# Split projections: a block's products with the high weights first, those with the low weights last

## The chip, the cores and the metric

One core of a Trainium2 chip runs the whole program. The metric is the device time of one execution in microseconds. Before the change it is 2193.56 us, the median of three runs (2186.81 to 2194.06).

## The reference

Two transformer-like blocks run one after the other on 256 rows of 1024 features, in 32-bit floats. The first block normalises its input and multiplies it with one wide matrix `w_in`; the parts feed an attention of eight heads, a gated delta rule of eight heads (short convolutions, and a triangular inverse in each chunk) and gates. Output projections, a gated feed-forward network of width 2816 and a small side embedding follow. The second block has two layers with 256 rows of context beside the 256 rows of input. Its first layer projects to a state-space scan and to a convolution of 31 taps (value times the sigmoid of a gate, then the taps per channel); its second layer is a gated linear recurrence in both directions. After each comes a mixture of 16 experts with a router. A normalisation ends it.

What matters here is the common core of all of these, a projection of rows x with weights W:

```python
y = x @ W      # x: 256 or 512 rows, K = 256 to 2816; W: K x N, all 32-bit floats
```

## The kernel before

**The split.** TensorE multiplies fp32r operands. To keep more digits, both operands of a projection are split into a high part (the value rounded to fp32r) and a low part (the value less its high part), and three of the four products are summed in one PSUM tile: high x by high W, low x by high W, high x by low W. `mm3` (L294 to L299) issues the three for one K tile of 128, one behind the other.

**Loading.** `load_split` (L262) fetches weights by one DMA of 512 KB on SP's queue into a tile `raw` (128 x 1024), copies it to `wh` on ScalarE (L271), and subtracts `wh` from it into `wl` (L276), on VectorE for two of three tiles and on GpSimd for the third. `wh` and `wl` have three buffers each, `raw` six. Such a tile holds four K tiles of two column blocks for the first kind of projection below (K = 1024), two K tiles of 512 columns for the second, so a group of work takes two or more of them.

**Two kinds of projection.** `proj_fm_steps` (L301) makes features by rows: 128 columns of W are the stationary operand and the rows x (T = 256 or 512) the moving one. It takes two blocks of 128 columns at a time when K is 1024: both halves of the weights are loaded, block 0 runs its eight K tiles of three products (24), block 1 its 24, then a consumer evicts each block. With T = 256 both blocks share a PSUM tile, with T = 512 each has its own. In all it makes 46 such pairs at T = 256: 20 in the first block's `w_in`, 22 in the feed-forward network and 4 in the last layer. `proj_tm_steps` (L327) makes rows by features: 128 rows of x are stationary and 512 columns of W move; for each K tile the loop goes over two or four row tiles, each with a PSUM tile of its own. It issues 608 triples of products in the program. The experts' own products run elsewhere (L2008 on), and the thin projections call `mm3` directly.

**Steps as filler.** Both are generators that yield after each `mm3`. Most callers run them through at once. Three draw steps in between other work. In the first block the triangular inverse runs in 6 levels by 4 groups (L663): four small matmuls, `fill()` (three steps of waiting projections), a ScalarE copy of their result, four matmuls on it, `fill()`, a predicated copy on VectorE, four transposes, `fill()`, another copy; the last level has no transposes, so there are 68 fills. In the state-space scan each of 16 chunk steps draws four steps of the z projection (L1297). In the second layer's output projection, normalisation pieces are put in between the steps (L1388).

**The order of the work.** The text gives each engine's instructions a priority, and the framework lays each engine's order out beforehand, by that priority and by the times at which it expects operands. So an instruction from further down stands ahead where an earlier one was expected late. On the chip each engine then runs its list strictly in that order. Writes to the same PSUM tile keep the order of the text. Convolution taps of the state-space layer are queued and placed a few at a time directly behind named instructions (`tick`, L972): 5 behind each subtraction on VectorE, 8 behind each eviction of a value block (L1101).

Of the kernel before, what the change touches and what calls it, by code (L numbers as in the profile page):

```python
# [18 lines left out]
P = 128  # L19
# [124 lines left out]
class Net:  # L144
# [149 lines left out]
    def mm3(self, out, lh, ll, rh, rl, start, stop):  # L294
# [3 lines left out]
        mm(out, lh, rl, start=False, stop=False)  # L298
        return mm(out, ll, rh, start=False, stop=stop)  # L299

    def proj_fm_steps(self, W, c0, nblk, x, T, consumer, tag="mm", bufs=3):  # L301


        K = W.shape[0] // P
        nb = 16 // K
        Wv = W.rearrange("(k p) n -> p k n", p=P)
        for b0 in range(0, nblk, nb):
            n = min(nb, nblk - b0)
            w = self.load_split(Wv[:, :, c0 + b0 * P:c0 + (b0 + n) * P], K, n * P)
            per = 512 // T  # L310
            ps = [self.psum(tag, bufs) for _ in range(-(-n // per))]
            for b in range(n):
                o = (b % per) * T
                s = slice(b * P, (b + 1) * P)
                for k in range(K):
                    wh, wl = w(k)
                    xh, xl = x(k)
                    yield self.mm3(ps[b // per][:, o:o + T], wh[:, s], wl[:, s], xh, xl, k == 0, k == K - 1)
            for b in range(n):
                o = (b % per) * T  # L320
                consumer(b0 + b, ps[b // per][:, o:o + T])
# [9 lines left out]
    def proj_tm_steps(self, W, c0, ncol, x, tiles, consumer, tag="mm", bufs=3, last=None, after=None):  # L331


        K = W.shape[0] // P
        Wv = W.rearrange("(k p) n -> p k n", p=P)
        for n0 in range(0, ncol, 512):
            ps = {t: self.psum(tag if i < 3 else "mx", bufs) for i, t in enumerate(tiles)}
            ws = {}
            end = last is not None and n0 + 512 >= ncol
            cut = K - LAST_K if end else K  # L340

            def products(k, t):
                if k not in ws:
                    kn = min(4, K - k)
                    w = self.load_split(Wv[:, k:k + kn, c0 + n0:c0 + n0 + 512], kn, 512)
                    ws.update({k + i: w(i) for i in range(kn)})
                ts = slice(t * P, (t + 1) * P)
                xh, xl = x(k)
                return self.mm3(ps[t], xh[:, ts], xl[:, ts], *ws[k], k == 0, k == K - 1)
            for k in range(cut):  # L350
                for t in tiles:
                    yield products(k, t)
            for group in last if end else (tiles,):
                for k in range(cut, K):
                    for t in group:
                        yield products(k, t)
                for t in group:
                    consumer(t, n0, ps[t])
                if after:
                    after(n0 // 512, group)  # L360
# [2182 lines left out]
```

## Time and profile before

| | |
|---|---|
| median of three runs | 2193.56 us |
| profiled execution | 2195.8 us, span 2194.0 us |
| mean granted TensorE clock | 0.959 |
| TensorE busy | 2011.8 us, 92% |
| VectorE busy | 1101.2 us, 50% |
| ScalarE busy | 870.1 us, 40% |
| GpSimd busy | 668.5 us, 30% |

The busy time of TensorE (PE) counts modelled ends of pipelined products: one with 512 columns stands as 0.39 us in a row, while the next starts 0.23 us later. So the distance between starts tells how fast products run, and the idle time in brackets tells how long the engine stood still and for what. PEld is the loading of the stationary operand, which runs beside the products. In an operand's name `uh`, `fh`, `ev0h` are high parts of x and `ul`, `fl`, `ev0l` low ones; L297 is high by high. In proj_fm L298 is low x by high W; in proj_tm the stationary operand comes first in `mm3`, so there L298 carries the low weights and L299 the low x.

### The profile page before, as it was taken

The numbers are of one execution on the slowest core, as the hardware profiler recorded it, in microseconds if no ns is written. First come the engines' busy times: TensorE is split into PE (matmuls) and PEld (weight loads), VectorE is DVE, ScalarE is ACT, GpSimd is POOL, SyncE is SP. The second block draws the span as 40 slices with busy tenths as digits, with TensorE's granted clock in tenths as the row PEclk, the third lists the DMA queues.
The fourth block names the chain that finished last, engine by engine and source line by source line (L and its number), as shares of the span: only waits on it lengthen the run. The fifth ranks groups of instructions, "written<-read, shape, count | busy, mean of one in ns | idle before, by whom it ended". The sixth has DMA issues, their size and how long they took to land. (4 is left out here: it accounts for less than half of the span.)

```text
span 2194.0 us, 29919 instructions
## 1 busy us (share of the span) xinstructions
PE 2011.8 (92%) x11360; PEld 1449.9 (66%) x11360; DVE 1101.2 (50%) x1980; ACT 870.1 (40%) x1407; POOL 668.5 (30%) x527
## 2 busy tenths in 40 slices
PE   7999999989999878999989799998899999799996
PEld 6799877779976655677768636663487666644342
DVE  6655453554435774796466523331625565633322
ACT  5554355453334443565554123230335555311111
POOL 1413322224432275525655322221312223201110
PEclk9999999999999989999999799999999999899998
DMA  7534556667675024231124699998645234989993
GB/s 227 157 107 138 152 165 198 216 194 230 222 238 168 20 74 111 78 106 49 41 96 137 230 354 347 372 362 325 226 137 180 88 105 154 325 301 395 395 343 135
DMA packets 282845, 433.13 MB, mean 197 GB/s; under 512 B 33722, under 2 KB 159290, under 8 KB 282432
## 3 DMA queue, kind: packets, MB, share of 16 engines
q1 hardware_dynamic: 261696, 407.17, 55.3%
q10 hardware_dynamic: 16528, 10.12, 1.7%
q0 software_dynamic: 4464, 13.79, 1.7%
q8 instruction: 94, 1.54, 0.3%
q14 instruction: 63, 0.52, 0.1%
HBM read 420.17 MB, written 9.54 MB: 196 GB/s over the span
## 5 line engine op out<-in xcount | busy, mean ns | idle before, releaser
L271 ACT ACTIVATE wh<-raw 128x1024 fp32r<-128x1024 f32 x288 | 303.4, 1057 | 390.3 <-PE mm L298 146.1
L276 POOL TENSOR_TENSOR wl<-raw,wh 128x1024 fp32r<-128x1024 f32 x92 | 223.2, 2426 | 623.9 <-ACT wh L271 573.8
L276 DVE TENSOR_TENSOR wl<-raw,wh 128x1024 fp32r<-128x1024 f32 x196 | 257.5, 1316 | 298.1 <-ACT wh L271 295.1
L2017 PE MATMUL mm<-we,xs 128*64 128x512 f32 x832 | 197.4, 618 | 12.0 <-DVEq L2178 9.4
L2017 PEld LDWEIGHTS mm<-we,xs 128*64 128x64 f32 x832 | 62.2, 142 | 136.1 <-issue 119.0
L2033 DVE TENSOR_TENSOR hh<-mm,hh 128x512 f32<-128x512 f32 x19 | 13.1, 692 | 210.9 <-PE mm L2017 148.5
L1144 DVE SCALAR_TENSOR_TENSOR cf<-us,cols,cf 128x200 f32<-128x200 f32 (+14 forms) x180 | 106.9, 659 | 0.1
L1132 POOL TENSOR_TENSOR cf<-cf,cfp 128x241 f32<-128x241 f32 (+14 forms) x120 | 93.2, 812 | 35.6 <-ACT cfp L1130 35.6
L2032 ACT ACTIVATE hh<-mm 128x512 f32<-128x512 f32 x22 | 13.1, 598 | 223.5 <-PE mm L2017 161.3
L297 PE MATMUL mm<-fh,wh 128*128 128x256 f32 x352 | 100.9, 287 | 0.0
L299 PE MATMUL mm<-fh,wl 128*128 128x256 f32 x352 | 99.9, 284 | 0.9 <-POOL wl L276 0.9
L298 PE MATMUL mm<-fl,wh 128*128 128x256 f32 x352 | 99.5, 283 | 0.0
L297 PE MATMUL mm<-uh,wh 128*128 128x256 f32 x320 | 97.0, 303 | 0.0
L299 PE MATMUL mm<-uh,wl 128*128 128x256 f32 x320 | 92.4, 289 | 1.8 <-DVE wl L276 1.5
L298 PE MATMUL mm<-ul,wh 128*128 128x256 f32 x320 | 91.9, 287 | 0.0
L2003 POOL TENSOR_TENSOR h<-h,yz 128x512 f32<-128x512 f32 x16 | 24.8, 1555 | 219.6 <-DVE yz L2002 219.4
L916 PE MATMUL mx<-mraw,cs 128*32 128x256 f32 x768 | 72.7, 399 | 7.4 <-DMA mraw<-in_mod_w 7.4
L299 PE MATMUL mm<-ev0h,wl 128*128 128x512 f32 x160 | 65.1, 408 | 14.0 <-DVE wl L276 13.9
L297 PEld LDWEIGHTS mm<-fh,wh 128*128 128x128 f32 x352 | 67.4, 191 | 5.4 <-issue 5.4
L297 PE MATMUL mm<-ev0h,wh 128*128 128x512 f32 x160 | 66.0, 414 | 5.3 <-DVE c L1183 4.3
L299 PEld LDWEIGHTS mm<-fh,wl 128*128 128x128 f32 x352 | 67.4, 192 | 1.6 <-POOL wl L276 1.4
L298 PEld LDWEIGHTS mm<-fl,wh 128*128 128x128 f32 x352 | 67.5, 192 | 0.0
(968 smaller groups left out, 5236.8 us busy)
## 6 DMA issues: line engine op xcount, KB each, us to landing
mraw<-in_mod_w SPq DMA_DIRECT2D x96, 512.0 KB
we<-in_moe_w_gate SPq DMA_DIRECT2D x37, 1024.0 KB
raw<-in_w_in SPq DMA_DIRECT2D x72, 512.0 KB
we<-in_moe_w_down SPq DMA_DIRECT2D x35, 1024.0 KB
we<-in_moe_w_up SPq DMA_DIRECT2D x32, 1024.0 KB
we<-in_moe_w_up SPq DMA_DIRECT2D x52, 512.0 KB
we<-in_moe_w_down SPq DMA_DIRECT2D x46, 512.0 KB
we<-in_moe_w_gate SPq DMA_DIRECT2D x42, 512.0 KB
```

The lines of the kernel that those rows point to most:

```text
L271: ins = nc.scalar.activation(hi, raw, AF.Copy)
L276: ins = eng.tensor_tensor(lo, raw, hi.bitcast(F32), ALU.subtract)
L297: mm(out, lh, rh, start=start, stop=False)
L298: mm(out, lh, rl, start=False, stop=False)
L299: return mm(out, ll, rh, start=False, stop=stop)
L916: nc.tensor.matmul(ps[32 * g:32 * g + 32, d:d + 256], self.cs[:, k, :], w[:, g, :], start=(k == 0), stop=(k == 7))
L1132: nc.gpsimd.tensor_tensor(a, a, s, ALU.add)
L1144: yield lambda a=a, s=s, j=j: nc.vector.scalar_tensor_tensor(a, s, w(j), a, op0=ALU.mult, op1=ALU.add)
L2003: (nc.gpsimd if d else nc.vector).tensor_tensor(x[:, t, ds], x[:, t, ds], z, ALU.add)
L2017: nc.tensor.matmul(out[r], x[0][:, k, r], w, start=start, stop=stop)
L2032: nc.scalar.activation(hh, pg[2 * i], AF.Silu)
L2033: nc.vector.tensor_tensor(hh, pg[2 * i + 1], hh, ALU.mult)
```

## The change

In proj_fm a block now runs all K tiles with the high weights first (high x and low x, through the new helper `mm3_high`), and then all K tiles with the low weights. It yields after each pair but the last, and once after the low products, so as often as before: seven steps of two products and one of ten. In proj_tm the same is done inside one K tile, over the row tiles: two products with the high weights for each row tile, then one with the low weights for each. The number of steps stays. Weights are loaded and consumers called at the same places of the text.

```diff
+    def mm3_high(self, out, lh, rh, rl, start):
+        self.nc.tensor.matmul(out, lh, rh, start=start, stop=False)
+        return self.nc.tensor.matmul(out, lh, rl, start=False, stop=False)
...
+                out = ps[b // per][:, o:o + T]
                 for k in range(K):
-                    wh, wl = w(k)
-                    xh, xl = x(k)
-                    yield self.mm3(ps[b // per][:, o:o + T], wh[:, s], wl[:, s], xh, xl, k == 0, k == K - 1)
+                    ins = self.mm3_high(out, w(k)[0][:, s], *x(k), k == 0)
+                    if k < K - 1:
+                        yield ins
+                for k in range(K):
+                    ins = self.nc.tensor.matmul(out, w(k)[1][:, s], x(k)[0], start=False, stop=(k == K - 1))
+                yield ins
...
-            def products(k, t):
+            def products(k, group):
                 if k not in ws:
...
-                ts = slice(t * P, (t + 1) * P)
-                xh, xl = x(k)
-                return self.mm3(ps[t], xh[:, ts], xl[:, ts], *ws[k], k == 0, k == K - 1)
+                mm = self.nc.tensor.matmul
+                wh, wl = ws[k]
+                xh, xl = [[v[:, t * P:(t + 1) * P] for t in group] for v in x(k)]
+                for i, t in enumerate(group):
+                    mm(ps[t], xh[i], wh, start=(k == 0), stop=False)
+                    ins = mm(ps[t], xl[i], wh, start=False, stop=False)
+                    if i < len(group) - 1:
+                        yield ins
+                for i, t in enumerate(group):
+                    ins = mm(ps[t], xh[i], wl, start=False, stop=(k == K - 1))
+                yield ins
             for k in range(cut):
-                for t in tiles:
-                    yield products(k, t)
+                yield from products(k, tiles)
             for group in last if end else (tiles,):
                 for k in range(cut, K):
-                    for t in group:
-                        yield products(k, t)
+                    yield from products(k, group)
```

## Rows read from the trace of the kernel before

**Rows 1.** Page part 1: engine, busy us (share of the span), instructions.
```profile
PE 2011.8 (92%) x11360; PEld 1449.9 (66%) x11360; DVE 1101.2 (50%) x1980; ACT 870.1 (40%) x1407; POOL 668.5 (30%) x527
```

**Rows 2.** Timeline in the inversion, all engines: start, us, line, out<-in, [idle before].
```profile
149.98 0.37 PE L297 MATMUL mm<-uh,wh 128*128 128x256 f32 x1
...
150.26 0.60 ACT L673 ACTIVATE U<-g 128x512 f32<-128x512 f32 x1 [0.37 <-PE g L670]
...
151.89 0.36 PE L297 MATMUL mm<-uh,wh 128*128 128x256 f32 x1
...
152.17 0.75 DVE L678 COPY_PREDICATED V<-k_first,g 128x512 f32<-128x512 uint8 x1 [1.14 <-PE g L676]
...
152.33 0.28 PE L297 MATMUL mm<-uh,wh 128*128 128x256 f32 x1
...
152.45 0.28 PE L298 MATMUL mm<-ul,wh 128*128 128x256 f32 x1
...
153.04 0.60 PE L682 MATMUL tr<-k_main,V 128*128 128x128 f32 x4
```

**Rows 3.** Timeline of PE around its longest wait for a low part.
```profile
788.04 0.39 PE L297 MATMUL mm<-ev0h,wh 128*128 128x512 f32 x1
788.26 0.39 PE L298 MATMUL mm<-ev0l,wh 128*128 128x512 f32 x1
802.58 0.80 PE L299 MATMUL mm<-ev0h,wl 128*128 128x512 f32 x1 [13.92 <-DVE wl L276]
...
813.57 0.39 PE L298 MATMUL mm<-ev1l,wh 128*128 128x512 f32 x1
813.80 0.39 PE L299 MATMUL mm<-ev1h,wl 128*128 128x512 f32 x1
```

**Rows 4.** Line 276: what its engines waited for, then who waited for it.
```profile
  ACT wh L271: 868.8, 174
...
  PE mm L299: 2.1, 1
...
  PE mm L299: 18.9, 7
```

**Rows 5.** Waits of PE: line, waited for, us in total, times, longest.
```profile
PE mm L299 <- DVE wl L276: 15.4, 2, 13.9
...
PE tr L1243 <- POOL xw L1241: 5.8, 6, 2.4
...
PE mm L299 <- POOL wl L276: 3.5, 5, 1.5
```

**Rows 6.** Line 299: weight loads, ns min/median/max.
```profile
L299 PEld LDWEIGHTS mm<-wh,ul x128: 187/188/330, 228.5 to 372.4; 128*128 128x128 f32 x128
```

**Rows 7.** Timeline of DVE in the same stretch.
```profile
792.09 0.68 DVE L1101 TENSOR_TENSOR us<-mm,cfg 128x512 f32<-128x512 f32 x1
792.69 8.21 DVE L1144 SCALAR_TENSOR_TENSOR cf<-us,cols,cf 128x248 f32<-128x248 f32 x8
800.82 1.71 DVE L276 TENSOR_TENSOR wl<-raw,wh 128x1024 fp32r<-128x1024 f32 x1
...
805.05 1.21 DVE L276 TENSOR_TENSOR wl<-raw,wh 128x1024 fp32r<-128x1024 f32 x1
```

**Rows 8.** Timeline of ACT in the same stretch.
```profile
791.85 1.06 ACT L271 ACTIVATE wh<-raw 128x1024 fp32r<-128x1024 f32 x1 [4.78 <-DMA raw<-in_ab_w_in]
```

**Rows 9.** Stretch behind the wait: busy us by engine, PEclk, DMA share, GB/s.
```profile
802.50:814.00 11.50, 11.42 (x44) 9.37 (x45) 7.26 (x14) 3.32 (x5) 2.14 (x3) 0.87 0.45 137
```

**Rows 10.** Groups by line in 470 to 690 us: busy, mean ns, idle before.
```profile
L271 ACT ACTIVATE wh<-raw 128x1024 fp32r<-128x1024 f32 x68 | 71.9, 1059 | 120.8 <-PE mm L298 64.4 <-PE mm L299 38.9 <-issue 12.7
...
L276 POOL TENSOR_TENSOR wl<-raw,wh 128x1024 fp32r<-128x1024 f32 x22 | 52.7, 2398 | 107.6 <-ACT wh L271 107.6
```

**Rows 11.** Groups by line in 117 to 235 us, PE.
```profile
L676 PE MATMUL g<-V,U 128*128 128x128 f32 x168 | 22.4, 276 | 0.0
...
L682 PE MATMUL tr<-k_main,V 128*128 128x128 f32 x76 | 11.7, 277 | 0.1
```

## The prediction, made before the result was known

> **What bounds the kernel now.** I read the page's busy times first, then the waits of TensorE over the whole span, then the line of the subtraction that makes the low weights, then the timeline at its longest wait. The reader is to see this. TensorE is busy 92% of the span, and has as many weight loads as products [rows 1], so the time is first of all a count of products. Products of the split projections are issued 0.12 us apart at 256 columns (152.33 to 152.45 us, [rows 2]) and 0.23 us apart at 512 (813.57 to 813.80, [rows 3]), whichever of the three operand pairs they carry. What the change can touch beside the count is time in which TensorE stands still for a low part: 18.9 us in 7 waits, as seen from the subtraction's line [rows 4], and 13.9 us of that is one wait [rows 5]. Everything else that TensorE waits for is named by other lines.
>
> **The change part by part.** Times are summed on the profiled execution, 2195.8 us (span 2194.0 and 1.8 around it); the median of the three timed runs is 2193.56, 2.2 below, and I subtract that at the end.
>
> (a) Count. No product, subtraction, copy, DMA or eviction is added or removed. A block of eight K tiles still has 24 products. At equal spacing that is 0 us.
>
> Here a rule of the Trainium skill speaks against the change. In proj_tm the stationary operand is the row slice of x: before, the high slice served two products in a row; after, the other slice comes between. The row to look at is 11360 loads for 11360 products [rows 1]: each product has its own load already, of 188 ns (median) in proj_tm [rows 6], shorter than the 0.23 us from product to product. The Trainium skill's page "TensorE: Matmul & The Clock Gate", section "Part 2: What happens when you issue a matmul", says that load and compute are separate so that weights are loaded once and used repeatedly. If that were so here, 608 triples of proj_tm would lose one shared load each, 608 x 0.188 = 114 us as an estimate from that row, if nothing covered it. By the row it is 0, and I take 0.
>
> (b) The 13.9 us wait. Two gate blocks are due. TensorE has issued the high pair of the first block's first K tile, and at 788.04 and 788.26 that of the next block; the low product follows only at 802.58 [rows 3]. Inside a block nothing else could go ahead, because the low product stood third in it. VectorE makes that low part at 800.82 to 802.53, behind the evictions of the value blocks with 8 convolution taps behind each (792.69 for 8.21 us) [rows 7]. The second half of the high weights was there early, at 791.85 + 1.06 = 792.91 [rows 8]; the second half of the low weights came at 805.05 + 1.21 = 806.26 [rows 7]. After the change 16 high products of the first block need no low part. If the order on TensorE is then strictly block by block, they run while it waits, but the second block's 24 products stay behind the first block's last four low ones: 28 x 0.227 = 6.4 us after 806.26, so the pair of blocks ends at 812.6 where it ended at 813.80 + 0.23 = 814.0: 1.4 us won. If the second block's 16 high products also go ahead, as its first two do now, 4 + 8 low products are left after 806.26, 2.7 us, and the pair ends at 809.0: 5.0 us won. I take 5.0: the low part stands on VectorE behind 8 taps that follow the last eviction, so the framework too must have expected it late, and 32 high products (7.3 us) fit into the 8.21 us of taps. The ends are 1.4 and the whole wait; a loss has no place, since nothing is made to wait longer. What is late next is the low parts themselves, from the same VectorE queue: of the 13.9 us some 7.5 stay before the first half (13.9 less 28 products) and some 2 come before the second (806.26 less 802.53 and 8 products).
>
> The clock: between 802.5 and 814.0 the granted clock is 0.87 [rows 9], some 11.5 x 0.13 = 1.5 us, a stretch at 1.2 GHz after the wait. As a wait of 7.5 us remains, I count none of this as won.
>
> (c) The other six waits, 18.9 - 13.9 = 5.0 us, the longest 1.5 [rows 4, 5]. A first low part is needed 14 products later in the block (place 17 instead of 3), 1.7 us at 256 columns and 3.2 us at 512, so each is covered. A second one is needed at 21 instead of 15, 0.7 us or 1.4 us later, which covers most. I count 4.0 won; ends 0 and 5.0.
>
> (d) Buffers. Each tag has three and a pair of blocks uses two, so the second half of the next pair reuses the first half's. Of the pair's 48 products the last reader of that high half moves from 36 to 32, that of the low half from 36 to 44. Now the subtraction waits for ScalarE's copy (868.8 us) and for a product's release hardly ever (2.1 us) [rows 4]; the copy, 1.06 us, waits for TensorE's releases [rows 10]. So at 256 columns it starts at about 36 + 9 = 45 products, and after the change at 44 + 1 = 45: no later, while the low part is needed 6 products, 0.72 us, later. GpSimd's 2.40 us [rows 10] then fit into 68 - 45 = 23 products, 2.76 us, where they had 17, 2.04. Cost 0; if GpSimd has other work in front of it, a piece half as long as its own, 1.2 us, the cover of 0.36 us is gone: 0.84 us for each of some 15 such parts (a third of 46 pairs), 13 us.
>
> (e) Steps used as filler. Both step functions yield as often as before, but in proj_fm seven steps now hold 2 products and the eighth 10, where each held 3. In the inversion (68 fills of three steps) five of eight fills shrink from 9 to 6 products, 1.08 to 0.72 us. The links that they cover: 149.98 to ScalarE's end at 150.86 plus 0.10 for the handover, 0.98 us, and 151.89 to 153.04 behind VectorE's predicated copy, 1.15 us [rows 2]. Uncovered would be 0.26 and 0.43 us: 24 x 5/8 x 0.26 + 20 x 5/8 x 0.43 = 9.3 us. The z projection in the scan loop alternates between 8 and 16 products per step of four instead of 12: eight short ones, 4 x 0.227 = 0.9 us each, 7.3 us. Together 16.6 us is the upper end; below nothing, -2 us, if the long fills cover more. But TensorE's order isn't the text's order: the runs of products between the inversion's matmuls in the trace aren't nines, and it waits 0.0 and 0.1 us before those matmuls [rows 11], so there I take 0. In the scan there is no such reserve: it already waits six times for GpSimd's xw [rows 5]; if half of these meet a short filler, 3 x 0.9 = 2.7 us lost, which I take.
>
> Sum: -5.0 - 4.0 + 0 + 2.7 = -6.3 us, 2189.5 on the profiled scale, **2187.3** against the median.
>
> **Rivals.** Faster: all low parts arrive in time, because high products fill the waits, or because VectorE's order puts the subtraction ahead of the taps. Then 18.9 + 1.5 us go: 2195.8 - 20.4 - 2.2 = 2173.2. For: TensorE bounds most stretches, so what is won stays won. Against: the taps are VectorE's own work, which no order of products shortens [rows 7]. It decides from 11 us won.
>
> Slower: the short fills lay bare the chains of the inversion and the scan. With (b) at its lower end, (c) lost and (e) in full: 2195.8 - 1.4 + 16.6 - 2.2 = 2208.8. For: the links, 0.98 and 1.15 us, are longer than six products. Against: TensorE hardly waits there [rows 11]. It is slower beyond doubt only when more than about 12 us of these 16.6 come true. The shared loads of (a) would end on this side too; 1 in 100, within this case.
>
> Not doing what it says: TensorE's order is laid out by expected readiness, so if the low parts were expected in time, the blocks keep their order and the wait only moves: 1.4 us, 2192.2.
>
> **How the numbers follow.** The forecast has 0.40 (its own range 2180 to 2195), the faster rival 0.28, no change 0.16, the slower one 0.16. Half of each outer rival left out, 0.16, gives the range 2170 to 2209. With 0.5% (11 us) as what can be told from no change, faster is below 2182.6 and slower above 2204.5: 0.28 and 0.05 of the forecast make 0.33; 0.15; the rest, 0.52, is the same.
>
> **What would show it.** In the profile after: the wait near 790 us for the low part is 7 to 8 us with some 32 high products ahead of it in a row (5.0), about 10 with 16 (1.4, rival three). The sum that TensorE waits for the low part falls from 18.9 to about 10. Subtraction and copy counts are unchanged, as are 120 and 227 ns between products; a longer spacing in proj_tm would prove (a) wrong. Waits of L670 to L682 stay under 1 us, those for xw rise by about 3. The prediction is wrong if time moves in stretches without a low-part wait, such as the feed-forward stage, or if the order of VectorE or GpSimd around the taps changes by tens of microseconds.

## The result, and the profile after

The changed kernel takes 2205.19 us (median of 16 runs, 2196.42 to 2215.35) where the kernel before takes 2193.45 (16 runs, 2182.48 to 2197.43) on the same chip: ratio 1.0057, 95% interval 1.0044 to 1.007. Another chip gave 1.0051 (1.0028 to 1.0074). It is slower by some 12 us; 6 us faster was forecast. The profiled execution took 2211.53 us.

The span and page part 1 of the changed kernel answer to [rows 1]: as many products and loads as before, on PE 5 us more of busy time in a span longer by 16.

```profile
span 2209.8 us, 29920 instructions
...
PE 2016.9 (91%) x11360; PEld 1454.3 (66%) x11360; DVE 1107.2 (50%) x1980; ACT 861.5 (39%) x1403; POOL 674.7 (31%) x527
```

The subtraction's line, changed kernel, answers to [rows 4]: what its engines waited for, and who waited for it. TensorE's wait for a low part (`PE mm`, second list) fell from 18.9 us to 9.9, as forecast. The subtraction now waits for a product to release its buffer 34 times instead of once.

```profile
its engine sat idle before it (us, times) until:
  ACT wh L271: 637.4, 132
  PE mm L327: 149.5, 34
...
who waited for it (us, times):
...
  PE mm L327: 9.9, 2
```

Waits of PE, changed kernel, with [rows 5]. L327 is the low product of proj_fm; L362, L363 and L367 are the three products of proj_tm. The lines to see are those of L362: the first product of a pass waits for evictions of the pass before (`va` and `v` by ScalarE, `oy` by VectorE). Of these three, only the one for `va` was there before, with 2.1 us, and it doesn't go with the order of the ends: with the last K tile back in the old order (below) it is 3.7 us, and in the changed kernel ScalarE stood idle ahead of this eviction until a DMA landed (last line, from the timeline). L1394 is taken up below.

```profile
PE mm L327 <- DVE wl L276: 8.5, 1, 8.5
...
PE mm L362 <- ACT va L672: 3.4, 1, 3.4
...
PE g L1394 <- DVE lnra L385: 5.5, 1, 5.5
...
PE mm L327 <- POOL wl L276: 1.4, 1, 1.4
...
PE mm L362 <- DVE oy L2465: 1.2, 1, 1.2
...
PE mm L362 <- ACT v L2298: 0.8, 1, 0.8
...
250.02 1.09 ACT L672 ACTIVATE va<-mm 128x512 f32<-128x512 f32 x2 [5.40 <-DMA mc<-md]
```

**The long wait** [rows 3, 7]. Timeline of PE in the changed kernel. From 794.74 to 799.72 go 23 high products, all 16 of the first block and 7 of the second, then the wait: 8.53 us where it was 13.92. Behind it the products are 0.43 us apart, not 0.23.

```profile
794.74 0.39 PE L303 MATMUL mm<-ev0h,wh 128*128 128x512 f32 x1
...
799.72 0.39 PE L303 MATMUL mm<-ev0h,wh 128*128 128x512 f32 x1
808.64 2.07 PE L327 MATMUL mm<-ev0h,wl 128*128 128x512 f32 x4 [8.53 <-DVE wl L276]
...
810.94 0.63 PE L303 MATMUL mm<-ev1h,wh 128*128 128x512 f32 x1
811.36 0.63 PE L304 MATMUL mm<-ev1l,wh 128*128 128x512 f32 x1
...
816.34 1.07 PE L327 MATMUL mm<-ev1h,wl 128*128 128x512 f32 x4
```

Timeline of DVE there: the same eight taps ahead of the same subtraction.

```profile
798.77 8.17 DVE L1161 SCALAR_TENSOR_TENSOR cf<-us,cols,cf 128x248 f32<-128x248 f32 x8
806.86 1.72 DVE L276 TENSOR_TENSOR wl<-raw,wh 128x1024 fp32r<-128x1024 f32 x1
```

**Where the time went: the end of a proj_tm pass.** In a pass with four row tiles each row tile's last product came three products after the previous one's, so the first could be evicted while the others still ran. Now the four last products follow one another. The clearest place is the second layer's output projection, where a normalisation fills in behind a pass. Timeline of all engines, kernel before. `yo` on ACT is the eviction; GpSimd multiplies it with the gate, VectorE adds it, and behind that stands the normalisation (`cft`), which TensorE needs at L1377. The pass's last product is the one at 1136.39, and the next pass's first could start 0.23 us later, at 1136.62: I count from there. The four `tr` of L1364 at 1137.30 come three products into the next pass.

```profile
1134.86 2.03 ACT L1348 ACTIVATE yo<-mm,ry 128x512 f32<-128x512 f32 x3 [2.42 <-PE mm L299]
1135.63 5.94 POOL L1349 TENSOR_TENSOR yo<-yo,m 128x512 f32<-128x512 f32 x4 [10.29 <-ACT yo L1348]
...
1136.39 0.39 PE L299 MATMUL mx<-wh,so1l 128*128 128x512 f32 x1
...
1136.95 3.46 DVE L1350 TENSOR_TENSOR xc<-xc,yo 128x512 f32<-128x512 f32 x2 [3.26 <-POOL yo L1349]
...
1137.30 0.60 PE L1364 MATMUL tr<-k_main,cf 128*128 128x128 f32 x4
1137.46 1.05 ACT L271 ACTIVATE wh<-raw 128x1024 fp32r<-128x1024 f32 x1
...
1147.47 0.69 PE L1377 MATMUL g<-k_main,cft 128*128 128x128 f32 x2 [3.61 <-DVE cft L1369]
```

The same place in the changed kernel (line numbers shifted by 17). The pass's last product is at 1143.21, so the next could start at 1143.44; here the transposes stand right there.

```profile
1142.79 1.06 ACT L271 ACTIVATE wh<-raw 128x1024 fp32r<-128x1024 f32 x1 [4.44 <-PE mx L363]
...
1143.21 0.39 PE L367 MATMUL mx<-wl,so1h 128*128 128x512 f32 x1
...
1143.44 0.93 PE L1381 MATMUL tr<-k_main,cf 128*128 128x128 f32 x7
1143.76 1.83 ACT L1365 ACTIVATE yo<-mm,ry 128x512 f32<-128x512 f32 x3
1143.92 2.39 POOL L276 TENSOR_TENSOR wl<-raw,wh 128x1024 fp32r<-128x1024 f32 x1 [10.65 <-ACT wh L271]
...
1146.27 5.91 POOL L1366 TENSOR_TENSOR yo<-yo,m 128x512 f32<-128x512 f32 x4
1147.60 3.47 DVE L1367 TENSOR_TENSOR xc<-xc,yo 128x512 f32<-128x512 f32 x2 [7.99 <-POOL yo L1366]
...
1156.32 0.90 PE L1394 MATMUL g<-k_main,cft 128*128 128x128 f32 x3 [5.45 <-DVE lnra L385]
```

The reader is to see two things. The high weights are released by the last high product (`mx L363`), four products before the pass ends, so their copy (1.06 us) now stands ahead of the evictions, and GpSimd's subtraction behind it (2.39 us) ahead of the gate; before, both came after. And the first eviction starts 0.32 us after the pass's end (1143.44) instead of 1.76 ahead of it (1136.62). So GpSimd's gate begins 2.83 us after the pass's end where it began 0.99 ahead, and TensorE takes up the normalised rows 12.88 us after it where it was 10.85.

The stretch around it, from the start of one product to the end of another, the same 635 products in each kernel: busy times by engine (the 636th is the one before, still running), and behind POOL the granted clock. First the kernel before, then the changed one. It takes 3.7 us longer, and TensorE stands still for 10.9 us of it (136.37 less 125.47) where it was 7.9. So this place shows 3.7 of the 15.8 us between the two profiles. The row of 130 to 220 us in each is for the inversion, below.

```profile
130.00:220.00 90.00, 89.95 (x786) 85.14 (x785) 47.88 (x84) 39.13 (x57) 28.35 (x20) 1.00 0.46 140
1095.95:1228.59 132.64, 124.74 (x636) 102.61 (x634) 80.22 (x108) 59.82 (x105) 70.11 (x51) 0.97 0.41 133
1147.50:1151.50 4.00, 4.00 (x16) 3.58 (x17) 3.16 (x6) 2.87 (x8) 0.57 (x2) 0.66 0.01 2
```

```profile
1156.00:1160.00 4.00, 3.68 (x14) 3.30 (x15) 2.70 (x5) 2.52 (x8) 1.94 (x2) 0.57 0.26 77
130.00:220.00 90.00, 88.64 (x755) 82.61 (x755) 46.36 (x78) 37.20 (x56) 28.39 (x18) 1.00 0.43 135
1101.59:1237.96 136.37, 125.47 (x636) 102.73 (x634) 78.46 (x108) 59.88 (x105) 67.88 (x51) 0.97 0.39 132
808.60:816.40 7.80, 7.76 (x22) 6.17 (x23) 4.87 (x11) 0.77 (x2) 0.00 (x0) 0.61 0.05 19
```

### The profile page after: what moved, and what is told of

The parts are those of the page before. It is cut to its first block, busy times and chain, and to the rows that moved or that the text cites. A ratio compares the mean times of both kernels' runs of the same rounds, so it can differ in the third digit from the quotient of the medians.

```text
span 2209.8 us, 29920 instructions
## 1 busy us (share of the span) xinstructions
PE 2016.9 (91%) x11360; PEld 1454.3 (66%) x11360; DVE 1107.2 (50%) x1980; ACT 861.5 (39%) x1403; POOL 674.7 (31%) x527
## 5 line engine op out<-in xcount | busy, mean ns | idle before, releaser
L276 POOL TENSOR_TENSOR wl<-raw,wh 128x1024 fp32r<-128x1024 f32 x92 | 232.5, 2528 | 636.3 <-ACT wh L271 415.9
L276 DVE TENSOR_TENSOR wl<-raw,wh 128x1024 fp32r<-128x1024 f32 x196 | 269.9, 1382 | 297.5 <-ACT wh L271 221.5
L303 PE MATMUL mm<-uh,wh 128*128 128x256 f32 x320 | 88.1, 305 | 0.2 <-ACT wh L271 0.2
L303 PE MATMUL mm<-fh,wh 128*128 128x256 f32 x352 | 87.5, 286 | 0.0
L304 PE MATMUL mm<-fl,wh 128*128 128x256 f32 x352 | 86.3, 283 | 0.0
L304 PE MATMUL mm<-ul,wh 128*128 128x256 f32 x320 | 83.6, 291 | 0.1
L303 PEld LDWEIGHTS mm<-uh,wh 128*128 128x128 f32 x320 | 62.5, 195 | 7.9 <-issue 7.0
L2034 PE MATMUL mm<-we,hT 128*64 128x512 f32 x208 | 60.9, 599 | 6.5 <-ACT hT L1915 6.5
L303 PE MATMUL mm<-ev1h,wh 128*128 128x512 f32 x160 | 65.4, 408 | 1.0 <-ACT wh L271 1.0
L304 PE MATMUL mm<-ev0l,wh 128*128 128x512 f32 x160 | 65.4, 409 | 0.0
```

What stands on the lines that cost most here:

```text
L276: ins = eng.tensor_tensor(lo, raw, hi.bitcast(F32), ALU.subtract)
L303: self.nc.tensor.matmul(out, lh, rh, start=start, stop=False)
L304: return self.nc.tensor.matmul(out, lh, rl, start=False, stop=False)
L2034: nc.tensor.matmul(out[r], x[0][:, k, r], w, start=start, stop=stop)
```

## Experiments

Each ratio is to the kernel before on the same chip, with its 95% interval.

**Which half: proj_fm alone, proj_tm alone.** The first takes the change out of proj_tm, the second out of proj_fm (it ran again later, beside the whole change); the first is the changed kernel with `products` again one triple of `mm3`, and

```diff
-                yield from products(k, tiles)
+                for t in tiles:
+                    yield products(k, t)
...
-                    yield from products(k, group)
+                    for t in group:
+                        yield products(k, t)
```

> Only proj_fm (features by rows) has the new order; proj_tm has the old one. Theory A, the loss sits in proj_tm, where the last products of all row tiles now stand next to each other at the end of a pass and their evictions come late: without it the kernel should be near 2195 us or below, ratio to before 0.997 to 1.001, as the 5 us won at the long wait stay. Theory B, the loss sits in proj_fm's uneven steps (2,2,..,10 products), which cover the chains of the inversion, the scan and the recurrence worse: ratio 1.003 to 1.006. Theory C, nothing but chance in the layout of the order: any value between 0.995 and 1.006.

> Only proj_tm (rows by features) has the new order; proj_fm has the old one, triple by triple. Theory A: the loss at the ends of passes stays, 4 to 6 us, ratio 1.002 to 1.004, with TensorE waiting for evictions at the starts of passes as in the changed kernel. Theory B: ratio 0.999 to 1.001. The wait of 13.9 us for a low part in the gate projection should be back in both.

> proj_tm changed alone, as before 1.0039. If the parts add, the whole change beside it is 0.002 quicker (proj_fm's win); if they cost more together, 0.002 slower.

> The whole change again, on the chip that runs the next kernel too. If its parts add up, 1.002; if they cost more together, 1.0057 again.

Measured: proj_fm alone 0.9981 (0.9964 to 0.9997), 4 us won; proj_tm alone 1.0039 (1.0023 to 1.0055) and again 1.0037 (1.0022 to 1.0051), 8 us lost. So the loss is proj_tm's. In the profile of proj_fm alone the long wait is as short as in the changed kernel:

```profile
PE mm L327 <- DVE wl L276: 8.6, 1, 8.6
```

**Is it the last K tile of a pass?** The changed kernel with the last K tile in the old order, and the kernel before with only the last K tile in the new one; then the latter beside the changed proj_fm.

```diff
             for k in range(cut):
+                if k == K - 1:
+                    yield from last_products(k, tiles)   # high pairs of all row tiles, then the low ones
+                    continue
                 for t in tiles:
                     yield products(k, t)
```

> The whole change, but proj_tm runs the last K tile of a pass in the old order, row tile by row tile, so that the first row tile's last product is again 3 products (two row tiles) or 9 (four) ahead of the last one's. Theory A: waits for evictions at starts of passes go back to those before, 4 us won, ratio 1.002 to 1.004 where the changed kernel has 1.0057. Theory B: as the changed kernel, 1.005 to 1.007.

> The kernel before, with the new order in one place alone: the last K tile of each pass of proj_tm (all products with the high weights, then one with the low weights for each row tile). Theory A, the row tiles end next to each other and their evictions come late: most of what proj_tm costs as a whole (ratio 1.0039), so 1.002 to 1.004. If the cost lies in the other K tiles or in the layout alone: 0.999 to 1.001.

> proj_fm changed, and of proj_tm the last K tile alone. If the two add, 0.9981 + 0.0036 = 1.0017. If the pass ends cost more beside the changed proj_fm, up to 1.0057, the time of the whole change.

Measured: 0.9998 (0.9979 to 1.0017) with the last K tile as it was, so 13 us of the changed kernel's time go; 1.0036 (1.0019 to 1.0052) with nothing but the last K tile changed, as much as all of proj_tm. Beside the changed proj_fm, 1.0007 (0.9991 to 1.0023): there the last K tile costs 0.0026, no more than by itself, and the whole change's 1.0057 isn't reached. The ends decide, but with both kinds changed the inner K tiles seem to take part too.

**Two row tiles or four.** The new order only in passes with four, and only in those with two.

```diff
+                if len(tiles) == 2:        # == 4 in the other kernel
+                    for i, t in enumerate(group):
+                        mm(ps[t], xh[i], wh, start=(k == 0), stop=False)
+                        mm(ps[t], xh[i], wl, start=False, stop=False)
+                        yield mm(ps[t], xl[i], wh, start=False, stop=(k == K - 1))
+                    return
```

> Old order in proj_fm; in proj_tm the new order only in calls with four row tiles (both halves of the state-space layer's output projection and the last layer's first projection), the old triples in calls with two. Theory A with the banks as its reason: a pass of four row tiles takes all four banks, so the next pass can't start before the first eviction, and there the first row tile's lead falls from 9 products (2.0 us) to 3 (0.7 us): ratio 1.001 to 1.003, the larger part of 1.0039. If the calls with two row tiles carry it: 0.999 to 1.001.

> Old order in proj_fm; in proj_tm the new order only in calls with two row tiles (10 of 13). Their lead falls from 3 products (0.7 us) to 1 (0.2 us). If four row tiles carry the cost: 0.999 to 1.001; if the two-tile calls do: 1.002 to 1.004. The two ratios of this pair should add up to about 1.0039 if the costs are independent; if they don't, it is the layout as a whole that costs.

Measured: four 1.0019 (1.0002 to 1.0035), two 1.0011 (0.999 to 1.0032). The shares can't be told apart; the second isn't told from nothing.

**More distance than before.** If ends too close together cost, ends further apart must win. The last two K tiles run row tile by row tile, so a row tile's last product comes six before the next one's; beside the changed proj_fm, and on the kernel before; then with the last four K tiles (twelve).

```diff
             for k in range(cut):
+                if cut == K and k >= K - 2:     # K - 4 for twelve
+                    continue
                 for t in tiles:
                     yield products(k, t)
+            if cut == K:
+                for t in tiles:
+                    for k in range(max(0, K - 2), K):
+                        yield products(k, t)
```

> New order in proj_fm, old triples in proj_tm, but in passes without split ends the last two K tiles run row tile by row tile: the first row tile then ends 6 products ahead of the next one instead of 3. Theory A, with the dose turned the other way: evictions start 0.7 us earlier still, and the kernel is 0 to 4 us faster than the one with proj_fm alone (ratio 0.9981), 0.996 to 0.998. If distance beyond 3 products is worth nothing, 0.998 to 0.999.

> The kernel before with one edit: in passes of proj_tm without split ends the last two K tiles run row tile by row tile (lead 6 products); proj_fm in the old order. Theory A: it wins by itself what the pair of kernels with proj_fm changed shows, 0.9944 / 0.9981 = 0.9963: expect 0.995 to 0.998. If it needs the new order of proj_fm: 0.999 to 1.001.

> As the run with the ends 6 products apart (0.9944), but the last four K tiles of a pass run row tile by row tile: 12 products (2.7 us) apart. An eviction takes 0.6 to 0.7 us and its handover some 0.3, so a lead of 1.4 us (6 products) should already cover it. Theory A then gives no more than 1 us beyond it: 0.993 to 0.996; if weight tiles held longer delay the next loads (three buffers, two tiles held), it falls back to 0.996 to 1.000.

Measured: 0.9944 (0.9922 to 0.9966), quicker than both kernels; 0.9979 (0.9965 to 0.9994) on the kernel before; twelve 1.0003 (0.9985 to 1.002). Timeline of the kernel with six at the same place as above. The pass's last product is at 1117.52, so its end by the same count is 1117.75. The first eviction starts 3.80 us ahead of that, the gate 3.03 ahead, and TensorE takes up the normalised rows 9.01 us after it.

```profile
1113.95 0.69 ACT L1364 ACTIVATE yo<-mm,ry 128x512 f32<-128x512 f32 x1 [0.38 <-PE mm L299]
...
1114.72 6.13 POOL L1365 TENSOR_TENSOR yo<-yo,m 128x512 f32<-128x512 f32 x4 [7.12 <-ACT yo L1364]
...
1117.52 0.39 PE L299 MATMUL mx<-wh,so1l 128*128 128x512 f32 x1
...
1118.01 0.69 ACT L1364 ACTIVATE yo<-mx,ry 128x512 f32<-128x512 f32 x1 [0.67 <-PE mx L299]
...
1118.44 0.60 PE L1380 MATMUL tr<-k_main,cf 128*128 128x128 f32 x4
1118.60 1.05 ACT L271 ACTIVATE wh<-raw 128x1024 fp32r<-128x1024 f32 x1
...
1126.76 0.66 PE L1393 MATMUL g<-k_main,cft 128*128 128x128 f32 x4 [1.74 <-DVE cft L1385]
```

Its stretches: the same 635 products, 132.64 and 136.37 us above, take 129.00, at full granted clock.

```profile
1126.70:1130.70 4.00, 3.94 (x23) 3.40 (x24) 3.27 (x8) 2.90 (x8) 0.54 (x1) 1.00 0.02 6
1075.93:1204.93 129.00, 122.06 (x636) 100.13 (x634) 79.02 (x108) 60.03 (x105) 67.37 (x50) 1.00 0.40 138
```

With twelve, waits of PE that no other kernel here has: proj_tm's low weights (L298) come late, since four K tiles' weights are now held until the last row tile.

```profile
PE mm L298 <- DVE wl L276: 2.8, 3, 1.6
PE mm L298 <- POOL wl L276: 1.8, 1, 1.8
```

These 4.6 us are the part of the fall from 0.9944 to 1.0003 (13 us) that the waits show; the rest isn't accounted for.

**The whole change with ends apart.** The changed kernel's products, its last two K tiles called with one row tile at a time.

```diff
+            if cut == K:
+                for t in tiles:
+                    for k in range(K - 2, K):
+                        yield from products(k, (t,))
```

> The whole change, but the last two K tiles of a proj_tm pass run row tile by row tile. If all of the loss sits in the ends, 0.994 as with the old order inside a pass. If changing the stationary operand at every product inside a pass costs something, 0.996 to 0.999.

Measured: 0.9962 (0.9945 to 0.998), 0.0095 quicker than the whole change. Whether the rest to 0.9944 is a cost of the inner order, the intervals don't tell. Its stretch, the same products again:

```profile
1086.68:1215.21 128.53, 122.05 (x636) 100.06 (x634) 77.78 (x108) 59.86 (x105) 66.77 (x51) 1.00 0.41 140
```

**Proj_fm by width, and its steps.** Proj_fm changed only at 512 columns, only at 256, the latter with a step after every three products; the whole change with such steps; and ends apart by six with proj_fm changed at 512 alone.

```diff
+                if not (T == 512):         # 256 in the other kernel
+                    for k in range(K):
+                        wh, wl = w(k)
+                        xh, xl = x(k)
+                        yield self.mm3(out, wh[:, s], wl[:, s], xh, xl, k == 0, k == K - 1)
+                    continue
...
                         ins = mm(out, w(k)[0][:, s], x(k)[i], start=(k == 0 and i == 0), stop=False)
+                        done += 1
+                        if done % 3 == 0:
+                            yield ins
```

> Old order in proj_tm; proj_fm has the new order only where it moves 512 columns (state-space layer, gates and values of the convolution, last layer's keys). It holds the 13.9 us wait of the prediction's steps (b) and the scan's shorter fillers of (e). By those steps: 5.0 + about 1.5 won, 2.7 lost, ratio 0.998 to 0.999; if the long wait gives back more, 0.996.

> Old order in proj_tm; proj_fm has the new order only where it moves 256 columns (first block and feed-forward network, one call in the last layer). By the prediction's steps (c) and (e): 2 to 2.5 us won, nothing lost in the inversion: ratio 0.999 to 1.000. If the short fills lay bare the inversion's chains (the slower rival), 1.002 to 1.004, most of it in 110 to 235 us.

> proj_fm changed at 256 columns alone (1.0024), with a step after every three products. If the short fills of the inversion are its cost, some 2.2 us come back: 1.0013. If the cost is elsewhere (later subtractions), 1.0024 again.

> The whole change, but proj_fm yields after every three products (eight steps of three, the order of products as in the changed kernel). Theory B: the chains are covered as before, the stretch of the inversion (110 to 235 us) gives back its 3.5 us and the whole falls to a ratio of 1.000 to 1.003. Theory A: no more than 1 us better than the changed kernel, ratio 1.004 to 1.006.

> As the ends six products apart (0.9944), with proj_fm changed at 512 columns alone. If the narrow blocks cost what they cost alone (1.0024), it is quicker still, 0.992. If their cost is only there beside a slow pass end, it stays at 0.994.

Measured: 512 columns 0.9981 (0.9963 to 0.9999), all that proj_fm wins; 256 columns 1.0024 (1.001 to 1.0037), and with even steps 0.9989 (0.9972 to 1.0005). So the uneven steps cost at 256 columns when proj_fm is changed there alone, more than the 2.2 us that I had put on them. The two widths don't sum (0.9981 and 1.0024 against 0.9981 for both), but the intervals are as wide as that difference. In the whole change even steps gave 1.0051 (1.003 to 1.0071), not told from 1.0057. Ends apart with 512 alone: 0.9935 (0.991 to 0.9959), the quickest, not told from 0.9944. In the inversion the stretch of 130 to 220 us holds 759 products with uneven steps, 773 with even ones, 786 before and 755 in the changed kernel; 31 products at 0.12 us are 3.7 us. The 14 that even steps bring back are 1.7 us, while the whole gained 0.0035, 7.7 us; where the rest came from isn't shown. First the kernel with 256 columns alone, then with even steps:

```profile
130.00:220.00 90.00, 88.66 (x759) 82.22 (x758) 47.36 (x79) 36.91 (x54) 28.76 (x19) 1.00 0.43 135
```

```profile
130.00:220.00 90.00, 89.13 (x773) 83.94 (x775) 46.44 (x80) 39.44 (x58) 27.05 (x18) 1.00 0.43 135
```

**One wait at every distance.** TensorE's waits in the normalisation's transposes of the four-row-tile pass (L1377 and its successors), summed in each profile, order these kernels: twelve apart 1.0 us; six 2.0 to 2.6 (four kernels); three, as before, 4.4 (seven kernels); the new last K tile alone 5.8 and 5.9; the whole new proj_tm there 6.2 to 6.3 (six profiles of four kernels). The stretch of the same 635 products orders them too: twelve apart 132.8 us; six 128.5 to 131.0; three 132.4 to 134.6; one, in the last K tile alone or in the whole new proj_tm, 135.8 to 138.2 (eight profiles). It is one place of many, but it moves with the distance, whatever proj_fm does; chance in the layout would hardly sort twenty profiles so.

## Why the prediction was wrong

**The step that failed is (a): "No product, subtraction, copy, DMA or eviction is added or removed ... At equal spacing that is 0 us."** The count was right, and so was the spacing. But for proj_tm this was the whole of the working: the order in which the row tiles finish their last products wasn't looked at, nor which product releases the high weights at a pass's end. Shown: that order alone, in the last K tile, gives 1.0036 on the kernel before; put back in the changed kernel it takes the loss away (0.9998); a wider one wins (0.9979 and 0.9944). Term (a) should have read about +8 us (1.0036 to 1.0039 of 2193). The rows for it stood in the profile: the eviction `yo` began 1.76 us before the pass's end, and ScalarE's copy came behind it. The prediction's own sign of error came true: time moved in stretches without a low-part wait. That 2205 us lies within the stated range of 2170 to 2209 is no merit: the time moved the other way than forecast.

**The rule on shared loads, weighed in (a), didn't come in.** The Trainium skill's page "TensorE: Matmul & The Clock Gate", section "Part 2: What happens when you issue a matmul", says that load and compute are separate so that weights can be loaded once and used repeatedly. In these traces no load was shared, before or after: the count of loads is 11360 in both, and proj_tm's products are 227 ns apart (median) in both traces.

**(b) The long wait: right in kind, 2.8 of 5.0 won.** High products of both blocks did go ahead. But 23 stood directly before the wait, not 32, as 9 of the second block's stayed behind it, so 8.53 us stayed, not 7.5; and the lower clock after it (0.61 over 7.80 us, 3.0 us lost, where [rows 9] gave 1.5) took more than I counted. The subtraction moved by 6.04 us from before to after and the pair's end, 816.34 + 4 x 0.227 = 817.25 against 814.03, by 3.22; the difference is what was won.

**(c) Right as to the waits.** Of the other six 1.4 us stays, so 3.6 went where 4.0 was counted; what that gave in time no run shows by itself. Proj_fm alone gives -4 us (interval -8 to -1) where (b) to (e) made -6.3.

**(d) Right in cost, not in kind.** "A product's release hardly ever" became 149.5 us, 34 times; but the low parts still came in time, since TensorE's waits for GpSimd's part fell from 3.5 us to 1.4.

**(e) Put in the wrong place.** I took 0 in the inversion and 2.7 us in the scan. The inversion lost some 3.7 us (31 products fewer in 90 us), and even steps gave about half back there; the scan's waits for `xw` stayed (5.8 before, 5.6 after). "TensorE's order isn't the text's order" was no reason for 0, and the waits of 0.0 and 0.1 us in [rows 11] couldn't show the cost: a filling product counts as busy for 0.28 us and the next can start after 0.12. In the changed kernel's 130 to 220 us seven starts of these matmuls (L693 and L699 there) stand 0.31 to 0.32 us behind the last filling product, and at most 0.04 of that counts as a wait; before, none stands so far behind. The one long wait there, 1.1 us, is for a convolution's output (L650).

**The slower rival** named short fills as its one mechanism; by them alone, 1.0024 at 256 columns, it would not have come about. That the time is near its 2208.8 is chance.

**What stays open.** The parts sum to 1.002, the whole is at 1.0057 and 1.0051: 0.003 to 0.004 more, 7 to 8 us, and not far outside what the intervals of these ratios leave open (on the second chip proj_fm alone wasn't run). The last K tile doesn't carry this excess (1.0007 beside proj_fm); the inner K tiles change the release order too, but no run shows how that costs only beside the changed proj_fm. Nor is it shown which of the two halves of the end, the later evictions or the earlier weight copy ahead of them, costs more: they weren't separated by a run. At the place shown above, as an estimate from its rows, the gate's delay of 3.8 us is 1.4 by the distance (six products of 0.227) and 2.4 by the copy and the subtraction that now stand ahead.

## What to carry to other kernels

When products over several accumulators are reordered, count where each accumulator's last product falls, and which product releases each weight buffer: the spacing of last products is the time that evictions have under cover, and an operand released early can let its refill jump ahead of the evictions on the same engine (seen in the timeline, not priced by itself). Here six products apart were better than three, one worse, and with twelve TensorE waited for weights, which were held too long. Work drawn as filler is better kept in equal pieces when its order inside changes: that paid at 256 columns alone, and couldn't be told in the whole change.

## What the runs showed of the hardware

The granted clock differs between these kernels: in the profiled executions its mean is 0.957 in the changed kernel, 0.959 before, 0.964 in the changed one with ends apart, and 0.970 with ends six apart beside the changed proj_fm. In the stretch of 635 products above, it is 0.97 before and 1.00 in the last of these, and TensorE's busy time for the same products falls from 124.74 to 122.06 us with it: of the 3.6 us won there, 2.7 are busy time and 1.0 waits. After the 5.45 us wait of the changed kernel the clock of the next 4 us is 0.57, so most of them ran at 1.2 GHz, the lower of its two levels; after the 3.61 us wait of the kernel before it is 0.66; after the 1.74 us wait with ends six apart it is 1.00, all at 2.4 GHz. So in this stretch a wait that was cut short gave more than its own length.

The Trainium skill's page "TensorE: Matmul & The Clock Gate", section "A second HAM failure mode: psum-queue depth-cycling", tells of a kernel whose short pauses between groups of products made the clock switch back and forth. The rows of this stretch agree in that the clock is full where the pauses are shorter; no run here changes the clock alone.
